# Sums of gated rows moved from the down projection of layer 1 to its up projection, and a query operand at another address

## The chip, the core and the metric

The kernel runs on one core of a Trainium2 chip. A core has a matrix engine (TensorE, PE in the profile), a vector engine (VectorE, DVE), a scalar engine (ScalarE, ACT), a general engine (GpSimd, POOL), a queue engine that here only issues transfers (SyncE, SP), an on-chip memory for operands (SBUF), accumulators that the matmuls write (PSUM), and DMA engines that move data between DRAM and SBUF. The metric is the device time of one execution in microseconds, the median of the runs.

## What is computed

Two transformer layers over 1024 tokens of width 1024, with 256 context tokens, in fp32. Layer 0 has a local attention, layer 1 grouped-query attention with rotary positions; both end in the same gated MLP with a depthwise convolution of width 3 over the tokens (2816 hidden channels per half, so 22 tiles of 128):

```python
def conv_ffn(x, w_up, conv_w, conv_b, w_down):
    h = x @ w_up
    h = lax.conv_general_dilated(h, conv_w[:, None, :], window_strides=(1,), padding=((1, 1),), ...
                                 feature_group_count=h.shape[-1]) + conv_b
    a, g = jnp.split(h, 2, axis=-1)
    return (jax.nn.silu(g) * a) @ w_down

for layer in range(DEPTH):
    xm = modulate(h, g_pre_m, sh_m, sc_m)
    y, yc = odd_mixer(...) if layer % 2 else even_mixer(...)
    h = h + gt_m * rms_norm(y, g_post_m)
    f = conv_ffn(modulate(h, g_pre_f, sh_f, sc_f), w_up[layer], conv_w[layer], conv_b[layer], w_down[layer])
    h = h + gt_f * rms_norm(f, g_post_f)
```

## The kernel before

The core works through the layers in order: attention, its output projection, up projection, down projection. In the last layer no context rows are carried, and only that layer is touched by the change.

**Precision.** An fp32 operand is split into a rounded part (hi) and the rest (lo); a product of two such operands is three matmuls, hi·hi, hi·lo, lo·hi. ScalarE casts the hi part (L121) and VectorE subtracts for the lo part (L122).

**Up projection** (`ffn_up`). It makes 22 hidden tiles j = 0 to 21, each of 128 channels by 1024 tokens, for the linear half and the gate half. Both halves together are written as a 2×2 block matrix and multiplied in seven half-sized products instead of eight: per tile 7 products × 4 blocks × 3 = 84 matmuls of 512 columns. The seven products need sums of weight blocks; GpSimd makes these, four operations of 128×512 per tile, into the single-buffered tile `sw` (L460, L461, L463, L464). VectorE adds up products (L479, L572), does the convolution in four steps of 128×1023 (L518, L519), and multiplies by the activated gate (L579); ScalarE starts the convolution and applies silu (L578). The tile is then stored to DRAM as `hid` j, 512 KB (L580, on SP's queue; the last tile's on ScalarE's).

**Down projection** (`ffn_down`). It multiplies hid with w_down by the same seven-product scheme. Its inner dimension is cut into three chunks of 3, 4 and 4 block pairs; the pair k consists of hid k and hid k + 11, each halved by tokens, which gives four blocks of 128×512: a11, a12 (first token half) and a21, a22 (second). They are loaded back from DRAM (L668, 256 KB each). In each chunk the products run in the order 1, 2, 5, 6, 7, 3, 4. Products 1, 2, 4 take plain blocks; 5, 6, 7, 3 take sums of them, made in place by GpSimd one product ahead, one operation of 128×512 per pair and product:

```python
def summed(name, s, i, e):
    if s:
        x, y, plus = s
        e.tensor_tensor(res[name][i], res[x][i], res[y][i], op=ALU.add if plus else ALU.subtract)   # L686
```

These are a21 + a22 for product 5, that minus a11 for 6, a12 minus the latter for 3, and a11 − a21 for 7. The sum is written over a block that an earlier product has split. Each product has four PSUM tiles of 4 (or 3) × 3 × 4 matmuls; ScalarE copies some of them out (L785, L796), VectorE adds the others to the rows y (L738 and like it), and GpSimd makes some additions of y in SBUF.

**Order.** A scheduler with a timeline of its own sets each engine's order from the program and its dependences; it runs before execution and the result is a fixed list for each engine. SP issues its loads and stores in that list's order and waits at each for its buffer or its data: weights (`wraw`, L445; `xm` for w_down, L653), hid stores and loads. Within the lists, what is written earlier in the program tends to stand earlier, and each engine executes strictly in its order.

**Attention of layer 1** (`odd_attn`). For each block of queries the scores are two accumulating matmuls per key tile (L1703): the keys' hi part with Q, and a second key operand with `q2`. `load_q2` (L1655) loads q2's lower 64 partitions; the tile is [128, 4, 128], 2048 bytes a partition, in three buffers.

Of the kernel before, what the change touches and what calls it, by code (L numbers as in the profile page):

```python
# [10 lines left out]
F32R = mybir.dt.float32r  # L11
AF = mybir.ActivationFunctionType
ALU = mybir.AluOpType
# [4 lines left out]
P = 128  # L18
T = 1024
# [8 lines left out]
NH = DFF // P  # L28
HF = 512
# [26 lines left out]
class Net:  # L56
# [415 lines left out]

        return [first, lambda: sums(1), lambda: sums(2), lambda: part(load(NH + j) if ctx else load(NH + j)[:, HF:])]

    def ffn_up(self, l, ctx, pre, zb, pool, side=None):

        nc = self.nc
        V, G = nc.vector, nc.gpsimd
        add = lambda o, x, y, e=V: e.tensor_tensor(o, x, y, op=ALU.add)  # L479
        order = [(0, 0), (0, 3)] if ctx else [(0, 0)]  # L480
        order += [(j, 0) for j in range(1, pre)]
        order += [(j, i) for j in range(NH) for i in range(4) if (j, i) not in order]
        steps = [self.up_weights(l, j, ctx, pool, 2 <= j < pre) for j in range(NH)]
        ready, state = {}, {}
        X, Xc = {}, []

# [37 lines left out]
        def one(j):  # L524

            a = take(j, 0)
            p1 = product(a[0], "B11")
            za = zt()
            nc.scalar.copy(za[:, HF:], p1)  # L529
            p2 = product(a[1], "B21")  # L530
            add(za[:, :HF], p2, za[:, HF:])
            oa = og = d = None
            rest = lambda: None
            if ctx:
                def rest():
                    conv(oa[:, T:], plain(a), j)
                if j == 0 or j >= pre:
# [47 lines left out]
        def run(X_, Xc_, hook1, hook2):  # L585
            X.update(X_)
            Xc.extend(Xc_ or [])
            for j in range(pre):
                one(j)
            for j in range(NH):  # L590
                if j >= pre:
                    one(j)
                if side:
                    self.steps(side, 1 if j % 4 else 2)
                if j == NH - 1:
                    hook1()
                two(j, hook2 if j == NH - 1 else None)

        return lambda: ahead(2), run

# [28 lines left out]
            self.tc.keep_in_program_order(nc.sync.dma_start(self.tD[l][k], r))  # L629
            yield  # L630

    def ffn_down(self, l, ctx, A, blocks, units):


        nc = self.nc
# [3 lines left out]
        chunks = [range(x, y) for x, y in zip(self.CUT, self.CUT[1:])]  # L639
        res = {}  # L640
        cnt = [0, 0, 0]

        def load_b(c, nm, pin):
            f = int(nm[1]) - 1
# [13 lines left out]
        def weights(n):  # L658

            if n < len(items):  # L660
                load_b(items[n][0], self.FORM[items[n][1]][1], 4 <= n < 7)

        def load_a(c, nm):
            r, h = int(nm[1]) - 1, int(nm[2]) - 1
            res[nm] = []
            for i, k in enumerate(chunks[c]):
                x = blocks(nm, i)
                nc.sync.dma_start(x, self.hidD[k + h * (NH // 2)][:, r * HF:(r + 1) * HF])  # L668
                res[nm].append(x)
            if ctx:  # L670
                n = len(chunks[c])
                x = blocks(nm, 4)[:, :n * P]
                nc.sync.dma_start(x.rearrange("p (k n) -> p k n", k=n), self.hidC[c][h][:, r])
                res[nm].append(x)

        def prep(c, nm):

            a, b, asum = self.FORM[nm]
            n = len(chunks[c])
            nu = n + (1 if ctx else 0)  # L680
            o = ops[c, nm] = [None] * nu, [None] * n

            def summed(name, s, i, e):
                if s:
                    x, y, plus = s
                    e.tensor_tensor(res[name][i], res[x][i], res[y][i], op=ALU.add if plus else ALU.subtract)  # L686

# [49 lines left out]
        def run(src, dst, sink):  # L737
# [101 lines left out]
            for n, (c, nm) in enumerate(items):  # L839
# [4 lines left out]
                for p in range(np_):  # L844
                    if p == 4:
                        for f in early + late:
                            f()
                        early = late = []
                    cnt[2] += 1
                    o = self.t(*((self.by, [P, HF], "by") if cnt[2] % 6 < 4 else (self.bj, [P, HF], "bj")))  # L850
                    multiply(o, c, nm, p, 0, len(chunks[c]))
                    collect(c, nm, p, o)
# [26 lines left out]
    def mlp(self, xa, opA, l, ctx, yT, w_out, src, mid, dst, ahead=None, after=None):  # L879
# [5 lines left out]
        A = lambda: self.t(xa, [P, HF], "xm", 16, F32R)  # L885
        mod = self.mod_cols(l, 1)
        halves = lambda x: x.rearrange("p (x n) -> p x n", x=2)
        with ExitStack() as e0:
            pool = lambda name, e: e.enter_context(tc.tile_pool(name=f"{name}{l}", reuse_waits="tile", bufs=1))
            xb = pool("xb", e0)  # L890

# [6 lines left out]
            with self.banks(out=4, turn=2):  # L898
              with self.banks(junk=1, tmp=1):
                with ExitStack() as e1:  # L900
                  xb2 = pool("xd", e1)
                  E = lambda dt=F32: self.t(xb2, [P, HF], "xd", 16, dt)
                  with ExitStack() as e2:
# [31 lines left out]
                      start, run = self.ffn_up(l, ctx, 2 if ctx else 6, 3 if ctx else 7, lambda: up[0], side)  # L935

                      def rows(n):
                          res = []
# [45 lines left out]
                  load_w, load_h, down = self.ffn_down(l, ctx, A, blocks, units)  # L984
                  with ExitStack() as e3:
                      up.append(pool("up", e3))

# [663 lines left out]

    def load_q2(self, pool, p, h, q):

        q2 = self.t(pool, [P, 4, P], "q2", 3, F32R)
        self.nc.sync.dma_start(q2[0:64].bitcast(F32), self.qP[p][0:64, h:h + 4, q * P:(q + 1) * P])  # L1655
        return q2

# [250 lines left out]
```

## Time and profile before

| | |
|---|---|
| median of 3 runs | 2901.68 us (2897.69 to 2901.73) |
| the profiled execution | 2902.14 us, span 2900.3 us, mean granted TensorE clock 0.989 |

Stages of the profiled execution, us from the span's start, with the busy time of each engine:

| stage | window | length | PE | DVE | ACT | POOL |
|---|---|---|---|---|---|---|
| attention, layer 1 | 1710 to 2133 | 423 | 413.87 | 330.33 | 232.57 | 372.46 |
| its output projection | 2133 to 2225 | 92 | 91.32 | 53.33 | 56.20 | 41.31 |
| up projection, layer 1 | 2225 to 2656 | 431 | 421.50 | 373.34 | 191.30 | 165.81 |
| down projection, layer 1 | 2656 to 2900 | 244 | 217.74 | 231.74 | 101.93 | 161.20 |

How to read the lines that follow: an instruction's row in the timeline is its start in us, its duration, engine, source line, operation, output and inputs by the program's names, shape, how many were joined, and in brackets how long its engine had been idle and what ended that. A group's row ends with the busy sum, the mean of one in ns, and the idle time before them. A row of the waits is the waiting engine, its tile and line, the engine and line that ended the wait, then the sum in us, the number, and the longest. A window's row has each engine's busy us (and count), the granted TensorE clock (1.00 is full), the busy share of the DMA engines and GB/s.

### The profile page before, as it was taken

What the parts mean: (1) busy time and instruction counts of PE and PEld (TensorE: products, weight loads), DVE (VectorE), ACT (ScalarE), POOL (GpSimd) and SP (SyncE); (2) the same over time, 40 slices, a digit from 0 to 9 for tenths busy, and PEclk for the clock granted to TensorE, in tenths of its full rate; (3) what the DMA queues carried; (4) which work ended last, traced back from release to release, by engine and by line L of the source; (5) the groups of instructions that cost most, each with busy time, mean ns of one, the idle gap of its engine ahead of it and who ended that gap; (6) DMA issues with size and microseconds to landing.
All of it is one profiled execution on the core that took longest, in us unless ns stands there. A gap on an engine that the chain in (4) does not pass through costs nothing.

```text
span 2900.3 us, 42828 instructions
## 1 busy us (share of the span) xinstructions
PE 2795.5 (96%) x15699; PEld 2252.0 (78%) x15699; DVE 2125.2 (73%) x2645; ACT 1330.5 (46%) x2373; POOL 1497.5 (52%) x1396
## 2 busy tenths in 40 slices
PE   8999999999999999999989999999998999999997
PEld 6878977776888888878768986666677878887775
DVE  4451255569776777798988768888856898888999
ACT  4321066575333333444457545555556444444443
POOL 2231277446222222165767768888864543332766
PEclk9999999999999999999999999999999999999998
DMA  8366773554223333464244562232253222224642
GB/s 314 127 209 211 242 270 133 197 188 151 79 96 124 118 102 109 167 204 129 75 138 155 148 180 93 101 102 99 84 204 138 73 95 88 88 80 168 202 142 87
DMA packets 235650, 413.89 MB, mean 143 GB/s; under 512 B 28320, under 2 KB 133792, under 8 KB 227504
## 3 DMA queue, kind: packets, MB, share of 16 engines
q1 hardware_dynamic: 212736, 395.61, 40.5%
q10 hardware_dynamic: 22704, 15.55, 1.8%
q8 instruction: 124, 2.03, 0.3%
q14 instruction: 86, 0.70, 0.1%
HBM read 306.16 MB, written 104.92 MB: 142 GB/s over the span
## 4 chain that ended last, share of the span: by engine, by line
PE 55%; DVE 11%; POOL 6%; issue 4%; ACT 2%; DMA 2%; SPq 0%; DVEq 0%; POOLq 0%; ACTq 0%
PE by L500 8%; PE by L501 8%; PE by L502 8%; PE b L1703 4%; PE by L1715 4%; PE b L1684 3%; PE by L877 2%; PE by L875 2%; PE by L876 2%; DVE xb L122 2%; DVE wlo L122 2%; PE by L509 1%; PE by L511 1%; PE by L510 1%; POOL rstd L139 1%
## 5 line engine op out<-in xcount | busy, mean ns | idle before, releaser
L1727 POOL TENSOR_TENSOR part<-part,pT 128x512 f32<-128x512 f32 x192 | 271.6, 1415 | 14.4 <-ACT pT L1704 1.0
L463 POOL TENSOR_TENSOR sw<-wraw,wraw 128x512 f32<-128x512 f32 x44 | 61.0, 1386 | 422.2 <-DVE wlo L122 422.2
L122 DVE TENSOR_TENSOR wlo<-wraw,whi 128x1024 fp32r<-128x1024 f32 (+1 forms) x162 | 221.1, 1371 | 77.4 <-ACT whi L121 77.3
L479 DVE TENSOR_TENSOR z<-by,z 128x512 f32<-128x512 f32 x264 | 176.7, 684 | 106.5 <-PE by L502 103.7
L1704 ACT ACTIVATE pT<-b 128x512 f32<-128x512 f32 x320 | 170.4, 604 | 151.2 <-PE b L1703 137.4
L1685 DVE TENSOR_REDUCE ng<-b 128x1 f32<-128x1280 f32 x122 | 181.7, 1490 | 75.7 <-PE b L1684 75.3
L121 ACT CAST whi<-wraw 128x1024 fp32r<-128x1024 f32 (+1 forms) x162 | 159.5, 990 | 160.8 <-PE b L310 107.0
L500 PE MATMUL by<-xb,whi 128*128 128x512 f32 x528 | 208.0, 394 | 1.7 <-ACT xb L121 1.7
L502 PE MATMUL by<-xb,wlo 128*128 128x512 f32 x528 | 205.9, 390 | 1.0 <-DVE wlo L122 1.0
L501 PE MATMUL by<-xb,whi 128*128 128x512 f32 x528 | 206.2, 391 | 0.3 <-DVE xb L122 0.3
L121 ACT CAST xb<-xb 128x512 fp32r<-128x512 f32 (+2 forms) x184 | 103.2, 567 | 195.2 <-PE by L876 61.6
L615 POOL TENSOR_TENSOR ts<-ts 128x512 f32<-128x512 f32 x88 | 118.3, 1352 | 134.9 <-DMA ts<-in_w_down_dram 133.2
L121 ACT CAST whi<-sw 128x1024 fp32r<-128x1024 f32 x88 | 92.5, 1052 | 202.6 <-PE by L501 173.6
L518 DVE SCALAR_TENSOR_TENSOR o<-z,cw,o 128x1023 f32<-128x1023 f32 x88 | 141.2, 1605 | 48.7 <-ACT o L517 48.6
L122 DVE TENSOR_TENSOR xb<-xb,xb 128x512 fp32r<-128x512 f32 (+2 forms) x184 | 158.9, 879 | 19.4 <-ACT xb L121 18.2
L517 ACT ACTIVATE o<-z,cw 128x1024 f32<-128x1024 f32 x88 | 109.6, 1245 | 130.5 <-DVE z L479 109.0
L460 POOL TENSOR_TENSOR sw<-wraw 128x512 f32<-128x512 f32 x44 | 80.6, 1832 | 167.6 <-DVE wlo L122 124.7
L738 POOL TENSOR_TENSOR y<-y,wraw 128x512 f32<-128x512 f32 x72 | 116.2, 1636 | 94.0 <-DVE wraw L738 59.3
L1715 PE MATMUL by<-pT,Vs 128*64 128x256 f32 x1280 | 150.7, 382 | 0.0
L500 PE MATMUL by<-xm,whi 128*128 128x512 f32 x352 | 138.5, 393 | 4.6 <-ACT z L529 3.2
L500 PE MATMUL by<-xd,whi 128*128 128x512 f32 x352 | 137.4, 390 | 0.4 <-DVE z L479 0.3
L501 PE MATMUL by<-xm,whi 128*128 128x512 f32 x352 | 137.5, 391 | 0.0
(314 smaller groups left out, 8922.0 us busy)
## 6 DMA issues: line engine op xcount, KB each, us to landing
wraw<-in_w_up_t_dram SPq DMA_DIRECT2D x92, 512.0 KB
awr<-in_w_ada_dram SPq DMA_DIRECT2D x44, 1024.0 KB
ts<-in_w_down_dram SPq DMA_DIRECT2D x44, 512.0 KB
tD<-ts SPq DMA_DIRECT2D x22, 1024.0 KB
xm<-tD SPq DMA_DIRECT2D x88, 256.0 KB
hid<-o SPq DMA_DIRECT2D x43, 512.0 KB
xm<-in_w_down_dram SPq DMA_DIRECT2D x66, 256.0 KB
xb<-hid SPq DMA_DIRECT2D x66, 256.0 KB
```

Source lines behind the costliest of these rows:

```text
L121: x = nc.scalar.copy(hi, src) if hi_eng == "s" else nc.vector.tensor_copy(hi, src)
L122: y = (nc.gpsimd if lo_eng == "p" else nc.vector).tensor_tensor(lo, src, hi.bitcast(F32), op=ALU.subtract)
L479: add = lambda o, x, y, e=V: e.tensor_tensor(o, x, y, op=ALU.add)
L500: nc.tensor.matmul(o, W[0][:, k, :], hi[k], start=(k == 0), stop=False)
L501: nc.tensor.matmul(o, W[0][:, k, :], lo[k], start=False, stop=False)
L502: nc.tensor.matmul(o, W[1][:, k, :], hi[k], start=False, stop=(k == 3))
L518: V.scalar_tensor_tensor(o[:, 1:], z[:, :n - 1], cw(0), o[:, 1:], op0=ALU.mult, op1=ALU.add)
L615: sub = lambda o, x, y: nc.gpsimd.tensor_tensor(o, x, y, op=ALU.subtract)
L1685: nc.vector.tensor_reduce(b["ng"][:, h:h + 1], ps[:, :S], axis=AX.X, op=ALU.max, negate=True)
L1704: nc.scalar.activation(b["pT"][:, k], ps, AF.Exp)
L1715: nc.tensor.matmul(out(b["po"][:, :256], i), self.KV[b["g"]][2][:, k], two(b["pT"][:, k], i), start=(k == 0), stop=(k == NT - 1))
L1727: nc.gpsimd.tensor_tensor(x, x if k > 1 else b["pT"][:, 0], b["pT"][:, k], op=ALU.add)
```

## The change

A generator `hidden_sums` is new. For each pair k it loads hid k and hid k + 11 into one tile `hs` of 128×2×1024 (single-buffered), makes the four sums in place with four GpSimd operations of 128×512, and stores the tile, 1 MB, to a DRAM buffer `sD` k. The up projection of layer 1 takes its tiles in the order 0, 11, 1, 12, …, 10, 21 so that pairs are complete early, and from the fourth tile on advances the generator by one or two steps per tile; the last two pairs' steps run into the down projection. There, `load_a` loads the block for product 5 from sD in place of a21, and `made` loads the blocks for products 6, 3 and 7 from sD, 33 loads of 256 KB, where GpSimd made sums before. Layer 0 is as it was. In the attention, q2's tile becomes 576 floats wide and the operand starts at its element 48, 192 bytes in.

```diff
+    def hidden_sums(self, l, pool):
+        nc = self.nc
+        e = lambda o, x, y, op=ALU.subtract: nc.gpsimd.tensor_tensor(o, x, y, op=op)
+        for k in range(NH // 2):
+            r = self.t(pool, [P, 2, T], "hs", 1)
+            for h in range(2):
+                nc.sync.dma_start(r[:, h], self.hidD[k + h * (NH // 2)])
+            yield
+            (x, y), (u, v) = ((r[:, h, :HF], r[:, h, HF:]) for h in range(2))
+            e(v, v, y, ALU.add)
+            e(y, x, y)
+            yield
+            e(x, v, x)
+            e(u, u, x)
+            nc.sync.dma_start(self.sD[l][k], r)
+            yield
+    SUM = {5: (1, 1), 7: (0, 1), 6: (0, 0), 3: (1, 0)}
...
-    def ffn_up(self, l, ctx, pre, zb, pool, side=None):
+    def ffn_up(self, l, ctx, pre, zb, pool, side=None, hs=None):
+        seq = [k + h * (NH // 2) for k in range(NH // 2) for h in range(2)] if hs else list(range(NH))
...
-                two(j, hook2 if j == NH - 1 else None)
+                late = hs and n > 2
+                if late and n % 2 == 0:
+                    next(hs)
+                two(j, hook2 if n == NH - 1 else None)
+                if late:
+                    next(hs)
...
+        def made(x, k, nm):
+            h, r = self.SUM[nm]
+            nc.sync.dma_start(x, sD[k][:, h, r * HF:(r + 1) * HF])
...
-                nc.sync.dma_start(x, self.hidD[k + h * (NH // 2)][:, r * HF:(r + 1) * HF])
+                if sD and nm == "a21":
+                    made(x, k, 5)
+                else:
+                    nc.sync.dma_start(x, self.hidD[k + h * (NH // 2)][:, r * HF:(r + 1) * HF])
...
-                if s:
+                if s and sD and i < n:
+                    if nm != 5:
+                        made(res[name][i], chunks[c][i], nm)
+                elif s:
...
+                    if hs and cnt[2] % 2:
+                        next(hs, None)
...
-        q2 = self.t(pool, [P, 4, P], "q2", 3, F32R)
+        q2 = self.t(pool, [P, 4 * P + 64], "q2", 3, F32R)[:, 48:48 + HF].rearrange("p (h q) -> p h q", h=4)
```

The instructions' order is the same on every engine up to the up projection of layer 1; inside it, it moves on POOL and SP alone; from its end on, on all of them. Line numbers below the new generator are 25 to 43 higher after.

**In the up projection, GpSimd.** Two tiles of the steady part; `sw` are the weight sums, `hs` the new tile. Before:

```order
L461 TENSOR_TENSOR sw_23145<-sw_23145,wraw_23123 128x512
L463 TENSOR_TENSOR sw_23145<-wraw_23123,wraw_23143 128x512
L464 TENSOR_TENSOR sw_23145<-wraw_23123,sw_23145 128x512
L460 TENSOR_TENSOR sw_23282<-wraw_23280 128x512
L461 TENSOR_TENSOR sw_23282<-sw_23282,wraw_23260 128x512
L463 TENSOR_TENSOR sw_23282<-wraw_23260,wraw_23280 128x512
```

After:

```order
L460 TENSOR_TENSOR sw_23462<-wraw_23460 128x512
L461 TENSOR_TENSOR sw_23462<-sw_23462,wraw_23440 128x512
L479 TENSOR_TENSOR hs_23684<-hs_23684 128x512
L463 TENSOR_TENSOR sw_23462<-wraw_23440,wraw_23460 128x512
L464 TENSOR_TENSOR sw_23462<-wraw_23440,sw_23462 128x512
L479 TENSOR_TENSOR hs_23684<-hs_23684 128x512 x3
L460 TENSOR_TENSOR sw_23602<-wraw_23600 128x512
L461 TENSOR_TENSOR sw_23602<-sw_23602,wraw_23580 128x512
L463 TENSOR_TENSOR sw_23602<-wraw_23580,wraw_23600 128x512
```

One new sum stands between the second and third weight sum of a tile, three more behind the tile's fourth, and the next tile has none.

**In the up projection, SP's queue.** `wraw` are the weights of a tile, `hid` its store, `hs` the load back for the sums, `sD` their store. Before:

```order
L580 DMA hid_7_4196_20886<-o_23059 128x1024
L445 DMA wraw_23280<-in_w_up_t_dram 128x1024
L445 DMA wraw_23397<-in_w_up_t_dram 128x1024
L580 DMA hid_8_4197_20887<-o_23196 128x1024
L445 DMA wraw_23417<-in_w_up_t_dram 128x1024
L445 DMA wraw_23534<-in_w_up_t_dram 128x1024
L580 DMA hid_9_4198_20888<-o_23333 128x1024
```

After:

```order
L605 DMA hid_5_4194_20884<-o_23513 128x1024
L483 DMA hs_23966<-hid_5_4194_20884 128x1024
L445 DMA wraw_23742<-in_w_up_t_dram 128x1024
L445 DMA wraw_23862<-in_w_up_t_dram 128x1024
L605 DMA hid_16_4205_20895<-o_23653 128x1024
L483 DMA hs_23966<-hid_16_4205_20895 128x1024
L445 DMA wraw_23882<-in_w_up_t_dram 128x1024
L445 DMA wraw_24004<-in_w_up_t_dram 128x1024
L492 DMA sD_5_4223_20915<-hs_23966 128x2048
L605 DMA hid_6_4195_20885<-o_23795 128x1024
```

Each tile's store is now followed by its load back, which waits for that store, and the next weights stand behind; one store of 1 MB comes per pair.

**At the end of the up projection, VectorE.** The last tile's convolution (o, z), last gate (o with o), and splits for the down projection: `xb` of hid blocks, `whi` and `wlo` of w_down. Before:

```order
L122 TENSOR_TENSOR xb_5013_25130<-xb_4987_25054,xb_5012_25129 128x512
L122 TENSOR_TENSOR wlo_25111<-xm_24914,wlo_25111 128x512
L122 TENSOR_TENSOR xb_5010_25115<-xb_4986_25052,xb_5009_25114 128x512
L572 TENSOR_TENSOR z_24982<-z_24982,by_25017 128x512
L518 SCALAR_TENSOR_TENSOR o_25013<-z_24888,cw_597,o_25013 128x1023
L122 TENSOR_TENSOR xb_5016_25145<-xb_4988_25056,xb_5015_25144 128x512
L519 SCALAR_TENSOR_TENSOR o_25013<-z_24888,cw_597,o_25013 128x1023
L518 SCALAR_TENSOR_TENSOR o_25031<-z_24982,cw_597,o_25031 128x1023
L519 SCALAR_TENSOR_TENSOR o_25031<-z_24982,cw_597,o_25031 128x1023
L122 TENSOR_TENSOR wlo_25239<-xm_24922,wlo_25239 128x512
L579 TENSOR_TENSOR o_25013<-o_25013,o_25031 128x1024
```

After:

```order
L122 TENSOR_TENSOR xb_4994_25065<-xb_4985_25045,xb_4993_25064 128x512
L122 TENSOR_TENSOR wlo_25202<-xm_25000,wlo_25202 128x512
L597 TENSOR_TENSOR z_25068<-z_25068,by_25103 128x512
L543 SCALAR_TENSOR_TENSOR o_25099<-z_24974,cw_597,o_25099 128x1023
L122 TENSOR_TENSOR xb_5034_25224<-xb_5008_25143,xb_5033_25223 128x512
L544 SCALAR_TENSOR_TENSOR o_25099<-z_24974,cw_597,o_25099 128x1023
L543 SCALAR_TENSOR_TENSOR o_25117<-z_25068,cw_597,o_25117 128x1023
L122 TENSOR_TENSOR xb_5031_25206<-xb_5007_25141,xb_5030_25205 128x512
L122 TENSOR_TENSOR xb_5037_25239<-xb_5009_25145,xb_5036_25238 128x512
L544 SCALAR_TENSOR_TENSOR o_25117<-z_25068,cw_597,o_25117 128x1023
L122 TENSOR_TENSOR wlo_25338<-xm_25008,wlo_25338 128x512
L604 TENSOR_TENSOR o_25099<-o_25099,o_25117 128x1024
```

The splits of the three blocks a12 of product 2 (before xb_4986 to 4988, after xb_5007 to 5009) stand otherwise among the steps L518 and L519 (L543 and L544 after): before, two ahead of the first step and one behind it; now all three behind it, two of them right ahead of the last step.

**At the down projection's sixth product in the first chunk, ScalarE.** Casts of hid blocks (`xb`) and weights, and the copies of product 5's PSUM tiles into y. Before, a_0 to a_2 are the blocks of product 6, summed by GpSimd, xb_4963 one of product 7, xb_4986 one of product 3:

```order
L121 CAST xb_5041_25262<-a_0_4989_25058 128x512
L121 CAST whi_25336<-xm_25081 128x512
L121 CAST xb_5044_25277<-a_1_4990_25060 128x512
L121 CAST wlo_25396<-xm_25148 128x512
L121 CAST xb_5058_25340<-xb_4963_24955 128x512
L121 CAST xb_5075_25420<-xb_4986_25052 128x512
L796 COPY y_0_4996_25072<-by_25228 128x512
L796 COPY y_1_4997_25073<-bj_25247 128x512
L796 COPY y_2_4998_25074<-bj_25266 128x512
L121 CAST xb_5047_25292<-a_2_4991_25062 128x512
L796 COPY y_3_4999_25075<-by_25281 128x512
```

After, a_0 to a_2 are the blocks of product 6, loaded from sD, and xb_5007 to 5009 those of product 3:

```order
L839 COPY y_0_5017_25161<-by_25327 128x512
L839 COPY y_1_5018_25162<-bj_25346 128x512
L839 COPY y_2_5019_25163<-bj_25365 128x512
L121 CAST xb_5097_25519<-xb_5007_25141 128x512
L121 CAST wlo_25495<-xm_25242 128x512
L121 CAST xb_5100_25535<-xb_5008_25143 128x512
L839 COPY y_3_5020_25164<-by_25380 128x512
L121 CAST whi_25499<-xm_25244 128x512
L121 CAST xb_5063_25361<-a_0_5010_25147 128x512
L121 CAST xb_5066_25376<-a_1_5011_25149 128x512
L121 CAST xb_5069_25391<-a_2_5012_25151 128x512
```

The casts of a_0 and a_1 stood ahead of the copies and that of a_2 ahead of the last one; now all three stand behind the last copy and one cast of weights, and two casts for product 3 stand ahead of them.

More of the change, by code (lines that the diff above doesn't have):

```diff
@@ L480, in ffn_up @@
         order = [(0, 0), (0, 3)] if ctx else [(0, 0)]
-        order += [(j, 0) for j in range(1, pre)]
-        order += [(j, i) for j in range(NH) for i in range(4) if (j, i) not in order]
-        steps = [self.up_weights(l, j, ctx, pool, 2 <= j < pre) for j in range(NH)]
+        order += [(j, 0) for j in seq[1:pre]]
+        order += [(j, i) for j in seq for i in range(4) if (j, i) not in order]
+        steps = {j: self.up_weights(l, j, ctx, pool, 2 <= n < pre) for n, j in enumerate(seq)}
         ready, state = {}, {}
@@ L536, in rest @@
                     conv(oa[:, T:], plain(a), j)
-                if j == 0 or j >= pre:
+                if j == 0 or j not in seq[:pre]:
                     oa = ot()
@@ L587, in run @@
             Xc.extend(Xc_ or [])
-            for j in range(pre):
+            for j in seq[:pre]:
                 one(j)
-            for j in range(NH):
-                if j >= pre:
+            for n, j in enumerate(seq):
+                if n >= pre:
                     one(j)
                 if side:
-                    self.steps(side, 1 if j % 4 else 2)
-                if j == NH - 1:
+                    self.steps(side, 1 if n % 4 else 2)
+                if n == NH - 1:
                     hook1()
-                two(j, hook2 if j == NH - 1 else None)
+                late = hs and n > 2
[4 more added lines that the diff above has]
+                    next(hs)
         return lambda: ahead(2), run
@@ L630, in down_sums, with ffn_down @@
             yield
-    def ffn_down(self, l, ctx, A, blocks, units):
+    def ffn_down(self, l, ctx, A, blocks, units, hs=None):
         nc = self.nc
@@ L641, in ffn_down @@
         cnt = [0, 0, 0]
+        sD = self.sD.get(l)
         def load_b(c, nm, pin):
@@ L887, in mlp @@
         halves = lambda x: x.rearrange("p (x n) -> p x n", x=2)
+        self.sD = {}
         with ExitStack() as e0:
+            hsum = None
+            if not ctx:
+                self.sD[l] = [self.t(self.dr, [P, 2, T], f"sD{l}_{k}") for k in range(NH // 2)]
+                hsum = self.hidden_sums(l, e0.enter_context(tc.tile_pool(name=f"hs{l}", reuse_waits="tile", bufs=1, side="right")))
             pool = lambda name, e: e.enter_context(tc.tile_pool(name=f"{name}{l}", reuse_waits="tile", bufs=1))
@@ L934, in mlp @@
                                                 acc=lambda: self.t(self.bj, [P, HF], "bj"), turn=lambda: self.t(self.bt, [P, 512], "b1"))
-                      start, run = self.ffn_up(l, ctx, 2 if ctx else 6, 3 if ctx else 7, lambda: up[0], side)
+                      start, run = self.ffn_up(l, ctx, 2 if ctx else 6, 3 if ctx else 7, lambda: up[0], side, hsum)
                       def rows(n):
@@ L983, in mlp @@
                   units = Units(lambda i: B(where[i]), len(where) // 2)
-                  load_w, load_h, down = self.ffn_down(l, ctx, A, blocks, units)
+                  load_w, load_h, down = self.ffn_down(l, ctx, A, blocks, units, hsum)
                   with ExitStack() as e3:
```

## The prediction, made before the changed kernel ran

> **What bounds the kernel now.** I read the page first, then the stages' windows, then what TensorE waits for in the last stage, then each of those waits in the timeline.
>
> ```profile
> PE 2795.5 (96%) x15699; PEld 2252.0 (78%) x15699; DVE 2125.2 (73%) x2645; ACT 1330.5 (46%) x2373; POOL 1497.5 (52%) x1396
> ```
> ```profile
> core 0: us, PE busy (x) PEld busy (x) DVE busy (x) ACT busy (x) POOL busy (x), PEclk, DMA share, GB/s
> 2440.40:2630.20 189.80, 189.80 (x839) 157.17 (x838) 159.12 (x161) 78.15 (x80) 63.75 (x40) 1.00 0.23 81
> 2656.00:2900.00 244.00, 217.74 (x928) 176.35 (x926) 231.74 (x260) 101.93 (x197) 161.20 (x112) 0.95 0.45 149
> 2660.00:2680.00 20.00, 16.54 (x66) 12.95 (x65) 17.31 (x19) 10.44 (x18) 6.32 (x4) 0.91 0.45 144
> 2680.00:2700.00 20.00, 17.63 (x76) 13.89 (x75) 20.00 (x18) 11.97 (x22) 15.03 (x9) 1.00 0.84 275
> 2780.00:2800.00 20.00, 18.13 (x73) 14.51 (x72) 20.00 (x19) 4.27 (x8) 17.69 (x11) 0.91 0.43 137
> ```
>
> TensorE (PE) is the bound as long as it is fed. The second row is ten hidden tiles in the steady part of layer 1's up projection: PE is busy all of the 189.80 us, VectorE 159.12, GpSimd 63.75. The third is layer 1's down projection to the end: VectorE 231.74 of 244, PE only 217.74. So the up projection has VectorE time to spare (30.7 us in ten tiles, 6.1 per pair) and PE none; in the down projection VectorE is full and PE waits for it. PE's waits from 2656 to 2900:
>
> ```profile
> PE by L875 <- ACT y L785: 3.5, 1, 3.5
> PE by L877 <- DVE xb L122: 2.7, 3, 1.6
> PE by L876 <- DVE whi L122: 1.9, 2, 1.1
> PE bj L876 <- DVE whi L122: 1.9, 1, 1.9
> PE by L876 <- DVE wlo L122: 1.3, 1, 1.3
> ```
> ```profile
> 2668.54 0.39 PE L877 MATMUL by<-wlo,xb 128*128 128x512 f32 x1
> 2672.39 0.50 PE L875 MATMUL by<-wlo,xb 128*128 128x512 f32 x1 [3.46 <-ACT y L785]
> ...
> 2690.54 0.74 PE L877 MATMUL by<-whi,xb 128*128 128x512 f32 x2 [1.55 <-DVE xb L122]
> 2696.23 0.72 PE L877 MATMUL by<-wlo,xb 128*128 128x512 f32 x2 [0.82 <-DVE xb L122]
> ...
> 2791.97 0.50 PE L876 MATMUL bj<-whi,xb 128*128 128x512 f32 x1 [1.87 <-DVE whi L122]
> ...
> 2792.91 0.63 PE L876 MATMUL by<-wlo,xb 128*128 128x512 f32 x1
> 2793.33 0.63 PE L877 MATMUL by<-wlo,xb 128*128 128x512 f32 x1
> ```
>
> 11.3 us of waiting, and more: after the long waits the granted clock falls (0.91 in 2660:2680 and in 2780:2800, so 0.09 x 20 = 1.8 us each), and matmuls start 0.42 us apart (2792.91, 2793.33). In all some 15 us that this stage could give back; the rest is fed PE or VectorE's closing work.
>
> **The sums, where they stand now.**
>
> ```profile
> L686 POOL TENSOR_TENSOR xb<-a,a 128x512 f32<-128x512 f32 x11 | 19.2, 1744 | 0.0
> L686 POOL TENSOR_TENSOR a<-a,a 128x512 f32<-128x512 f32 x11 | 19.0, 1750 | 24.5 <-DMA a<-hid 24.5
> L686 POOL TENSOR_TENSOR a<-a,xb 128x512 f32<-128x512 f32 x11 | 18.8, 1710 | 15.0 <-DVE xb L122 15.0
> L686 POOL TENSOR_TENSOR xb<-xb,a 128x512 f32<-128x512 f32 x11 | 18.3, 1666 | 0.0
> ```
> ```profile
> 2660.37 1.28 DVE L518 SCALAR_TENSOR_TENSOR o<-z,cw,o 128x1023 f32<-128x1023 f32 x1
> 2662.17 2.32 DVE L519 SCALAR_TENSOR_TENSOR o<-z,cw,o 128x1023 f32<-128x1023 f32 x1
> 2664.41 2.31 DVE L518 SCALAR_TENSOR_TENSOR o<-z,cw,o 128x1023 f32<-128x1023 f32 x1
> 2666.75 2.19 DVE L519 SCALAR_TENSOR_TENSOR o<-z,cw,o 128x1023 f32<-128x1023 f32 x1
> 2669.04 1.06 ACT L578 ACTIVATE o<-o 128x1024 f32<-128x1024 f32 x1 [4.21 <-DVE o L519]
> 2671.38 0.33 ACTq L580 DMA_DIRECT2D hid<-o  x1
> 2671.75 1.56 ACT L785 COPY y<-by 128x512 f32<-128x512 f32 x3 [1.15 <-DVE o L579]
> 2661.76 6.10 POOL L686 TENSOR_TENSOR a<-a,a 128x512 f32<-128x512 f32 x3 [24.48 <-DMA a<-hid]
> ```
>
> 44 GpSimd operations, 75 us, not on PE's path themselves. What they do to VectorE is. The same convolution step takes 1.28 us at 2660.37 and 2.32, 2.31, 2.19 once GpSimd's three sums run beside it (2661.76, 6.10 us): about 1.0 us of VectorE lost per sum. So the 44 cost VectorE up to 45 us of the 231.74.
>
> Price by wait, gains negative:
>
> 1. The wait at 2672.39 (3.46). PE wants a PSUM buffer; ScalarE frees it (L785, 2671.75) behind the last store of hid, which waits for the last gate, which waits for those three steps. Without sums beside them they end 1.04 + 1.03 + 0.91 = 3.0 us sooner. In the new order two splits, some 0.6 each like the copies of 2671.75 (1.56 for three), stand behind the steps that stood ahead of them, no net change. 0.5 us of wait stays and most of the clock's 1.8 goes. Ends -3.0 to -5.3; I take -4.5, nearer the second, since a wait of 0.5 is like the 0.82 at 2696.23, in a window at clock 1.00.
>
> 2. The waits at 2690.54 and 2696.23 (2.4 together). Nine sums ran there, four remain (the last pair's): five at 1.0 free more VectorE time than was waited for. New instead: ScalarE's cast of product 6's operand stands behind the copy of product 5's last PSUM tile and one other cast, so PE waits for copy, cast and cast, 3 x 0.6 = 1.8 us. Net -0.6; ends -2.4 (the wait is covered) and +2 (it drops the clock too).
>
> 3. The wait at 2791.97, 1.87 plus 1.8 of clock. VectorE was full from 2680 on with 16 sums beside it; without them it has 16 us more for a delay of 1.9. -3.2; ends 0 and -3.7.
>
> 4. The remaining 3.5 us of waits, almost all in the last two products. GpSimd's eight additions of y (L738) stay beside them. -1.0; ends 0 and -3.5.
>
> 5. 33 sums become loads of 256 KB on SP's queue, written over a block that the product before has to have split.
>
> ```profile
> SPq L653 <- DMA hid<-o: 14.6, 1, 14.6
> ```
> ```profile
> 2674.01 1.27 SPq L653 DMA_DIRECT2D xm<-tD  x3
> ```
>
> The store issued at 2671.38 lets SP go on at 2674.01: 2.6 us from issue to landing for 512 KB, and I take that for a load too. A product of four blocks lasts 48 x 0.227 = 10.9 us, so a load is hidden if SP issues it in the product's first half. SP is in order, and one late load holds the weights behind it. The other 11 loads stand in place of loads of a21. +1.0; ends 0 and +5.
>
> 6. The up projection gets 40 of the 44 sums (the last pair's four run in the down projection), 20 loads of 512 KB, ten stores of 1 MB.
>
> ```profile
> 2444.34 1.29 POOL L463 TENSOR_TENSOR sw<-wraw,wraw 128x512 f32<-128x512 f32 x1 [7.90 <-DVE wlo L122]
> 2450.97 1.68 POOL L460 TENSOR_TENSOR sw<-wraw 128x512 f32<-128x512 f32 x1 [4.08 <-DVE wlo L122]
> ```
>
> GpSimd waits 7.90 and 4.08 us in each tile for VectorE to release the buffer of weight sums: one new sum falls into the first gap of one tile in two and three into the second, where 3 x 1.3 = 3.9, or 3 x 2.2 when contended. The latter delays L460 by some 2.5 us; behind it wait ScalarE's cast and a product that was prepared more than a product ahead. VectorE loses 4 x 1.04 = 4.2 us per pair and has 6.1. On SP each load of hid stands behind the store of the same tile and waits 2.6 us for it, with the next weights queued behind; before, those weights waited for GpSimd anyway. The order of tiles costs nothing: the same products, and all pairs of the first chunk are done long before. +1.0 for local lag; 0 is one end, +10 the other (1 us per pair; a gain is excluded, since PE has no wait there).
>
> 7. The query operand. No row shows addresses, so I go by starts of equal matmuls.
>
> ```profile
> 2440.29 0.39 PE L500 MATMUL by<-xb,whi 128*128 128x512 f32 x1
> 2440.51 0.39 PE L501 MATMUL by<-xb,whi 128*128 128x512 f32 x1
> ```
> ```profile
> 1905.10 0.40 PE L1703 MATMUL b<-q,k 128*128 128x512 f32 x1
> 1905.34 0.40 PE L1703 MATMUL b<-Q,k 128*128 128x512 f32 x1
> ```
>
> 0.22 to 0.23 us apart in the up projection, 0.24 in the attention. If the new place took that difference away for its 320 matmuls, 320 x 8 ns = 2.5 us; a loss of the same size I can't exclude. I take 0.
>
> Sum: -4.5 - 0.6 - 3.2 - 1.0 + 1.0 + 1.0 + 0 = -7.3. The profiled execution took 2902.14 us (span 2900.3), which gives 2894.8. The median of the runs is 0.5 lower (2901.68): **2894.4 us**.
>
> **Rivals.** A measurement of this kernel can tell 0.2%, 5.8 us, from no change.
>
> *The relief is given back* (no change). Loads of sums arrive late behind SP's in-order queue, and PE waits for casts where it waited for VectorE: term 5 at +5 and term 2 at +2 leave about -1, so 2901. For it: at 2680:2700 the DMA share is already 0.84. Against: it falls to 0.43 later. It decides if a load is issued after half a product.
>
> *VectorE becomes the bound of the up projection* (slower). It decides where four sums cost VectorE more than the 6.1 us per pair, 1.5 us each.
>
> ```profile
> L461 POOL TENSOR_TENSOR sw<-sw,wraw 128x512 f32<-128x512 f32 x15 | 32.4, 2158 | 1.2
> ```
>
> A contended GpSimd operation lasts 2158 ns; if VectorE stood still for all of that, 4 x 2.16 = 8.6, 2.5 us too much, times ten pairs +25: 2920 at the worst, 2908 at half of it. Against: 1.04 lost per sum is what 2662.17 to 2666.75 show. The Trainium skill, "SBUF — State Buffer", section "SBUF: two separate sides", speaks for it: GpSimd and a VectorE operation with two SBUF inputs take their shared ports as an exclusive lock for the whole instruction, and the other blocks fully. By that rule a sum could cost its full uncontended 1.29 us instead of 1.04: 5.2 per pair instead of 4.2, still below 6.1, so the sum stays, with less room; I give this rival a larger chance for it.
>
> *The query's place matters more* (faster): the attention's other matmuls gain too, -2.5 or more, 2892 and below.
>
> **How the numbers follow.** Forecast 0.55 (2890 to 2898; 0.48 of it beyond 5.8 us, 0.07 within), relief given back 0.22, up projection slower 0.15, query place 0.08. Faster 0.48 + 0.08 = 0.56; same 0.07 + 0.22 = 0.29; slower 0.15. Range 2888 to 2903: it takes in the given-back case whole, leaves out about 0.12 of the slow one and 0.08 below.
>
> **What would show it.** Right: no wait near 3.5 us at the first PSUM copies and none at the third chunk's start; VectorE's splits in the down projection shorter; the up projection as long as before within 2 us, its convolution steps slower. Wrong: PE waits for splits (DVE wlo, xb) inside the up projection; ScalarE's casts waiting for DMA of sD; the attention's stage longer or shorter by over 3 us.

## The result and the profile after

The changed kernel is slower: 2918.18 us (median of 4 runs, 2916.4 to 2920.66) against 2899.68 (4 runs); the ratio is 1.0067, 95% interval 1.0050 to 1.0084. The forecast was 2894.4, range 2888 to 2903.

The profiled execution has a span of 2915.2 us, 14.85 above the 2900.32 of before. I cut both at the same matmuls. A stage's length is counted from its first matmul's start to its last one's, and the down projection's from the last matmul of the up projection on. The four starts of the changed kernel:

```profile
2211.18 0.48 PE L525 MATMUL by<-xm,whi 128*128 128x512 f32 x1
2677.01 0.39 PE L527 MATMUL by<-xd,wlo 128*128 128x512 f32 x1
2677.24 0.39 PE L920 MATMUL by<-whi,xb 128*128 128x512 f32 x1
2898.85 0.39 PE L922 MATMUL by<-whi,xb 128*128 128x512 f32 x1
```

| | before | after | difference |
|---|---|---|---|
| attention, layer 1 | 413.17 | 407.39 | -5.78 |
| up projection | 437.93 | 465.83 | +27.90 |
| down projection | 228.33 | 221.83 | -6.50 |
| the rest | 1820.89 | 1820.12 | -0.77 |

So the up projection, put at +1, lost 28. The down projection came within 2 us of what the forecast's terms 1 to 5 sum to (-8.3), but by luck: a larger relief and a larger cost than forecast offset each other, as the account of terms 1 to 5 below shows. The same stretches by engine, first the up projection (437.93 and 465.83 us), then the down projection to the span's end; before:

```profile
2218.37:2656.30 437.93, 428.42 (x1880) 350.67 (x1879) 378.24 (x402) 195.41 (x234) 169.07 (x119) 0.99 0.27 95
2656.53:2900.31 243.78, 217.21 (x925) 175.94 (x923) 231.21 (x259) 101.93 (x197) 161.20 (x112) 0.95 0.44 148
```

and after:

```profile
2211.18:2677.01 465.83, 437.63 (x1880) 350.39 (x1879) 402.49 (x397) 191.57 (x235) 247.28 (x159) 0.99 0.37 132
2677.24:2915.16 237.92, 212.77 (x925) 174.34 (x923) 193.16 (x263) 101.10 (x196) 86.66 (x72) 0.96 0.59 202
```

VectorE (third busy time) went up by 24 us in the up projection for 40 sums (GpSimd has 159 operations there, 119 before), 0.6 us a sum, less than the 1.04 of the forecast; with 402 busy of 466 it is not the bound of that stage as a whole. What TensorE waits for there, in the steady part from 2400 to 2660, is this; in the kernel before no wait is seen from 2400 to 2656:

```profile
PE by L525 <- DVE z L504: 6.0, 6, 1.0
PE by L525 <- ACT whi L121: 4.4, 6, 0.9
PE by L527 <- DVE wlo L122: 3.2, 6, 0.5
```

Three waits once per pair of tiles, each at the same place. One pair, GpSimd's timeline:

```profile
2441.03 2.15 POOL L461 TENSOR_TENSOR sw<-sw,wraw 128x512 f32<-128x512 f32 x1
2453.38 1.30 POOL L479 TENSOR_TENSOR hs<-hs 128x512 f32<-128x512 f32 x1 [10.19 <-issue]
2454.63 2.27 POOL L463 TENSOR_TENSOR sw<-wraw,wraw 128x512 f32<-128x512 f32 x1
2456.87 1.28 POOL L464 TENSOR_TENSOR sw<-wraw,sw 128x512 f32<-128x512 f32 x1
2458.12 5.22 POOL L479 TENSOR_TENSOR hs<-hs 128x512 f32<-128x512 f32 x3
2463.30 2.27 POOL L460 TENSOR_TENSOR sw<-wraw 128x512 f32<-128x512 f32 x1
2465.65 2.16 POOL L461 TENSOR_TENSOR sw<-sw,wraw 128x512 f32<-128x512 f32 x1
```

SP, VectorE and TensorE beside it:

```profile
2447.16 0.33 SPq L605 DMA_DIRECT2D hid<-o  x1
2449.82 0.33 SPq L483 DMA_DIRECT2D hs<-hid  x1
```
```profile
2449.05 1.22 DVE L122 TENSOR_TENSOR wlo<-sw,whi 128x1024 fp32r<-128x1024 f32 x1
2454.04 1.72 DVE L544 SCALAR_TENSOR_TENSOR o<-z,cw,o 128x1023 f32<-128x1023 f32 x1
2459.26 1.23 DVE L122 TENSOR_TENSOR wlo<-sw,whi 128x1024 fp32r<-128x1024 f32 x1 [3.50 <-ACT whi L121]
2460.41 1.78 DVE L122 TENSOR_TENSOR wlo<-wraw,whi 128x512 fp32r<-128x512 f32 x1
2462.11 2.31 DVE L543 SCALAR_TENSOR_TENSOR o<-z,cw,o 128x1023 f32<-128x1023 f32 x1
2464.94 1.71 DVE L544 SCALAR_TENSOR_TENSOR o<-z,cw,o 128x1023 f32<-128x1023 f32 x1
2466.58 2.32 DVE L122 TENSOR_TENSOR wlo<-wraw,whi 128x1024 fp32r<-128x1024 f32 x1
```
```profile
2459.29 0.50 PE L525 MATMUL by<-xb,whi 128*128 128x512 f32 x1 [0.68 <-ACT whi L121]
2460.55 0.50 PE L527 MATMUL by<-xb,wlo 128*128 128x512 f32 x1 [0.53 <-DVE wlo L122]
2469.55 0.50 PE L525 MATMUL by<-xd,whi 128*128 128x512 f32 x1 [0.98 <-DVE z L504]
```

Read it from GpSimd. It is free at 2443.2. VectorE releases `sw` at 2450.27 (2449.05 + 1.22), and the tile's third weight sum L463 could run then. But a sum of hidden rows stands ahead of it, and that one waits for its rows: the tile's store is issued at 2447.16, the load back 2.66 us later, and the sum starts at 2453.38, 3.56 us after that. (The row names no releaser for it, only "issue"; but in nine of the ten pairs the first sum starts 3.4 to 3.6 us after its load is issued.) L463 starts at 2454.63, 4.4 us late. The cast of these weights comes late, VectorE stands idle 3.50 us for it, and TensorE waits 0.68 and 0.53 us. Then VectorE has to catch up while three sums and the next tile's L460 and L461 run beside it: its steps take 2.31, 1.71, 2.32 us, and TensorE waits 0.98 us for a PSUM tile. From start to start of their 168 matmuls, a pair of tiles lasts 41.2 us in place of 38.1.

In the down projection the waits of before are gone, all but one of 1.7 us and two under 0.4, and one is new, 7.0 us before product 6 (below it, a wait of SP's queue):

```profile
PE by L920 <- ACT xb L121: 7.0, 1, 7.0
PE by L920 <- ACT y L828: 1.7, 1, 1.7
```
```profile
SPq L685 <- DMA hid<-o: 6.2, 1, 6.2
```
```profile
2698.74 1.27 SPq L685 DMA_DIRECT2D xm<-tD  x3
2700.05 1.38 SPq L685 DMA_DIRECT2D xm<-in_w_down_dram  x3
2701.47 0.43 SPq L483 DMA_DIRECT2D hs<-hid  x1
2701.95 1.91 SPq L685 DMA_DIRECT2D xm<-tD  x3
2704.04 2.05 SPq L698 DMA_DIRECT2D a<-sD  x3
2706.43 6.65 SPq L685 DMA_DIRECT2D xm<-in_w_down_dram  x8
```
```profile
2711.35 1.97 ACT L121 CAST xb<-a 128x512 fp32r<-128x512 f32 x3 [2.66 <-DMA a<-sD]
```
```profile
2704.67 0.39 PE L922 MATMUL by<-whi,xb 128*128 128x512 f32 x1
2712.02 0.80 PE L920 MATMUL by<-wlo,xb 128*128 128x512 f32 x1 [6.96 <-ACT xb L121]
```
```profile
2704.00:2711.00 7.00, 1.06 (x5) 0.56 (x3) 5.38 (x6) 4.64 (x9) 3.01 (x3) 0.88 1.01 339
```

SP stands for 6.2 us until the last hid store has landed. Then it issues ten other loads, and product 6's three blocks are asked for from 2704.04 on, when product 5's last matmul (2704.67) is about to start. The cast that needs them starts at 2711.35, 7.3 us later. In between, from 2704 to 2711, the DMA engines are busy all the time (share 1.01) and TensorE 1.06 us of 7.

### The profile page after: what moved, and what is told of

It reads as the page before. It is cut to its first block, busy times and chain, and to the rows that moved or that the text cites. A ratio compares the mean times of both kernels' runs of the same rounds, so it can differ in the third digit from the quotient of the medians.

```text
span 2915.2 us, 42936 instructions
## 1 busy us (share of the span) xinstructions
PE 2798.1 (96%) x15699; PEld 2251.1 (77%) x15699; DVE 2106.6 (72%) x2645; ACT 1326.0 (45%) x2373; POOL 1504.2 (52%) x1396
## 4 chain that ended last, share of the span: by engine, by line
PE 50%; DVE 12%; issue 6%; POOL 6%; DMA 4%; ACT 3%; DVEq 0%; POOLq 0%; ACTq 0%; SPq 0%
PE by L525 5%; PE by L527 5%; PE by L526 5%; PE b L1754 5%; PE by L1766 4%; PE by L920 3%; PE by L922 3%; PE by L921 3%; DVE wlo L122 3%; PE b L1735 3%; DVE o L543 2%; PE bj L920 1%; PE bj L921 1%; PE bj L922 1%; PE by L534 1%
## 5 line engine op out<-in xcount | busy, mean ns | idle before, releaser
L122 DVE TENSOR_TENSOR wlo<-wraw,whi 128x1024 fp32r<-128x1024 f32 (+1 forms) x162 | 235.8, 1461 | 79.4 <-ACT whi L121 79.4
L463 POOL TENSOR_TENSOR sw<-wraw,wraw 128x512 f32<-128x512 f32 x44 | 68.0, 1545 | 340.7 <-DVE wlo L122 340.7
L504 DVE TENSOR_TENSOR z<-by,z 128x512 f32<-128x512 f32 x264 | 176.5, 683 | 89.4 <-PE by L527 86.2
L1736 DVE TENSOR_REDUCE ng<-b 128x1 f32<-128x1280 f32 x122 | 181.9, 1491 | 75.6 <-PE b L1735 75.3
L543 DVE SCALAR_TENSOR_TENSOR o<-z,cw,o 128x1023 f32<-128x1023 f32 x88 | 142.6, 1621 | 49.4 <-ACT o L542 49.2
L460 POOL TENSOR_TENSOR sw<-wraw 128x512 f32<-128x512 f32 x44 | 84.4, 1917 | 133.9 <-DVE wlo L122 91.8
```

Source lines behind the costliest of these rows:

```text
L122: y = (nc.gpsimd if lo_eng == "p" else nc.vector).tensor_tensor(lo, src, hi.bitcast(F32), op=ALU.subtract)
L543: V.scalar_tensor_tensor(o[:, 1:], z[:, :n - 1], cw(0), o[:, 1:], op0=ALU.mult, op1=ALU.add)
L1736: nc.vector.tensor_reduce(b["ng"][:, h:h + 1], ps[:, :S], axis=AX.X, op=ALU.max, negate=True)
```

## The experiments

Twelve runs. "Attention", "up" and "down" are the lengths in us of the three stages in the run's profile, cut as in the table above. The ratio is the run's time to that of the kernel before, measured beside it, with its 95% interval. Line numbers are those of each run's own kernel. First the cause in the up projection and the place of q2, each part alone.

**q2_only**: the kernel before with

```diff
-        q2 = self.t(pool, [P, 4, P], "q2", 3, F32R)
+        q2 = self.t(pool, [P, 4 * P + 64], "q2", 3, F32R)[:, 48:48 + HF].rearrange("p (h q) -> p h q", h=4)
```

> The kernel before with the moved query operand alone. Between the first and the last score matmul the attention of layer 1 took 413.2 us before and 407.4 after the whole change. Theory (the place of q2 gives this): attention 407 to 408, all else as before, time 5 to 6 us below before. Rival (only the matmuls that follow q2 gain, 3.3 ns each, 320 of them): 1 us less, not distinguishable from before. Rival (chance between executions): attention 412 to 414.

Attention 407.1; ratio 0.9983 (0.9973 to 0.9992). This looked like the theory; the later runs below say otherwise.

**sums_only**: the changed kernel with that line as before.

> The changed kernel with q2 back in its old place: the sums' move alone. Theory: up projection (first to last matmul) 466 us against 437.9 before, down projection (from there to the last matmul) 222 against 228.3, attention 413: time 20 to 22 us above before. Rival (q2's place gives nothing): 15 to 18 above, as the whole change.

Ratio 1.0085 (1.0069 to 1.0100), which is 25 us of 2899 (20 to 29), at or above the 20 to 22 of the theory and more than the rival's 15 to 18. Up 468.1, down 222.1 as in the whole change, and attention 409.5, shorter than the 413.2 of before although q2 is in its old place. So the loss is the sums' move, and something other than q2 moves the attention's time.

**behind**: all four sums of a pair pinned behind the last weight sum.

```diff
-                nc.gpsimd.tensor_tensor(s1, A12, s1, op=ALU.subtract)
+                self.sw_last = nc.gpsimd.tensor_tensor(s1, A12, s1, op=ALU.subtract).ins
...
-            e(v, v, y, ALU.add)
-            e(y, x, y)
+            with self.tc.issue_after(self.sw_last):
+                e(v, v, y, ALU.add)
+                e(y, x, y)
```

> The changed kernel with all four sums of a pair queued behind the tile's last weight sum, so that the first of them, which waits for its load, no longer stands ahead of two weight sums. Theory (the wait for the load ahead of the weight sums costs 0.86 + 0.69 = 1.55 us per pair, the sums' contention with VectorE 1.15): up projection 466 - 15 = about 451 us. Rival (VectorE's lost time alone is the cause): 466, unchanged. Rival (SP's queue delays weights): 466, unchanged.

Up 455.0, ratio 1.0028 (1.0018 to 1.0038). The steady pairs went from 41.2 to 39.1 us, so the wait ahead of the weight sums cost 2.05 us a pair, more than the 1.55 read off the waits; two of the first tiles got 2 to 3 us longer, which is why the stage gained 10.9 and not 15. Both rivals expected no change. From 2400 to 2660 only VectorE's lateness is left, about one wait per pair:

```profile
PE by L526 <- DVE z L505: 5.5, 7, 1.0
PE by L528 <- DVE wlo L122: 0.8, 1, 0.8
```

Yet VectorE is busy for longer than in the changed kernel, 414.86 us against 402.49, in a stage that is 10.9 us shorter, so the time that VectorE loses in all does not set the stage's length:

```profile
2208.52:2663.49 454.97, 432.71 (x1881) 350.93 (x1879) 414.86 (x398) 192.54 (x235) 257.04 (x159) 0.99 0.39 135
```

**no_sums**: the loads and stores stay, the GpSimd operations go.

```diff
-            e(v, v, y, ALU.add)
-            e(y, x, y)
...
-            e(x, v, x)
-            e(u, u, x)
```

> The changed kernel without the four GpSimd operations of a pair: the loads of hid and the stores to sD stay, so sD holds plain rows and the result is not the reference's. Theory and the rival of VectorE's lost time: up projection 438 to 440 us, as before. Rival (loads and stores on SP's queue delay the weights): 460 to 466. The down projection keeps its wait of 7 us for the loads of product 6 if that is a matter of the loads; if it is due to the last pair's sums, it goes.

Up 437.7, ratio 0.9947 (0.9934 to 0.9959). The 20 loads, ten stores and the new order of tiles cost TensorE nothing; all 28 us come from the GpSimd operations. The down projection (218.8) kept a wait of 6.7 us for product 6's cast: that one is a matter of the loads.

Then the two repairs, alone and together.

**spread**: two sums behind the last weight sum of one tile, two behind the first two of the next. The generator also starts one tile earlier and takes two steps per pair instead of three.

```diff
-                nc.gpsimd.tensor_tensor(s1, s0, A11, op=ALU.subtract)
+                self.sw_mid = nc.gpsimd.tensor_tensor(s1, s0, A11, op=ALU.subtract).ins
...
+            with self.tc.issue_after(self.sw_last):
                 e(v, v, y, ALU.add)
                 e(y, x, y)
             yield
+            with self.tc.issue_after(self.sw_mid):
                 e(x, v, x)
                 e(u, u, x)
             nc.sync.dma_start(self.sD[l][k], r)
-            yield
...
-                late = hs and n > 2
-                if late and n % 2 == 0:
-                    next(hs)
+                if hs and n > 1:
+                    next(hs)
                 two(j, hook2 if n == NH - 1 else None)
-                if late:
-                    next(hs)
```

> The changed kernel with the same sums of a pair in two halves: two behind the last weight sum of one tile, two behind the first weight sums of the next tile, where GpSimd waits longest. All four queued together behind the last weight sum left the up projection at 455.0 us against 437.7 without the sums, 1.05 us per pair in the steady part. Theory (what remains is VectorE late at one place, since three to four sums run beside it in a row): with two at a time its spare time of 3.1 us per tile covers them, up projection 440 to 445, time near 2895. Rival (each sum costs TensorE in proportion, wherever it stands): 455, as with four together.

Up 448.0; ratio 1.0004 (0.9994 to 1.0014). In the steady part no wait for another engine is left, and a pair lasts 38.6 us in place of 38.1. The stage still misses the forecast by 3 to 8 us: tiles four to seven, counted from zero at 84 matmuls in a row each, take 86.8 us against 79.8 before.

**early6**: the changed kernel, product 6's sums loaded into the blocks of a22, which are free from the start of the chunk, and a22 loaded behind product 6.

```diff
-                if sD and nm == "a21":
-                    made(x, k, 5)
+                if sD and nm in ("a21", "a22"):
+                    made(x, k, 5 if nm == "a21" else 6)
...
-                    if nm != 5:
+                    if nm in (7, 3):
...
+            if sD and nm == 6:
+                a = "a22"
...
+                elif sD and nm == 4 and i < n:
+                    nc.sync.dma_start(res[name][i], self.hidD[chunks[c][i] + NH // 2][:, HF:])
```

> The changed kernel with the loads of product 6 into the block of a22, free long before, and a22 itself (needed by product 4) loaded behind product 6. Theory (the wait of 7.0 us before product 6's matmuls comes from its loads, which stand in SP's queue behind loads that wait, and then share the DMA engines): the wait goes and with it the clock's loss behind it, down projection 222 - 7 to 9 = 213 to 215 us, time 2909 to 2911. Rival (the loads are late wherever they go, since the DMA engines are full): a wait of 5 us or more stays, 220 to 222.

Down 212.6, ratio 1.0039 (1.0027 to 1.0051). The wait of 7.0 is gone, and what is left of TensorE's waits in the whole stage is

```profile
PE by L924 <- ACT y L832: 1.7, 1, 1.7
PE by L926 <- DVE xb L122: 0.3, 1, 0.3
PE bj L926 <- DVE xb L122: 0.3, 1, 0.3
```

SP now issues the three loads of the first chunk with three others from 2692.28 on, ahead of its wait for the last hid store and of the ten loads behind that. 9.2 us from product 6's loads issued earlier: 7.1 between two matmul starts (2704.67 and 2712.02, over the usual 0.227), and 2.1 of slow starts that followed.

**spread6**: both.

> Both of the above. Theory: up projection 440 to 445, down projection 213 to 215, attention 407: time 2884 to 2890, 10 to 15 us below before. Rival (the gains meet in one place, the start of the down projection): no better than the first of the two, near 2895.

Up 448.0, down 212.6, as the two alone; ratio 0.9989 (0.9980 to 0.9997). The time, 2899.0, is above the 2884 to 2890 expected. The up projection stayed above 440 to 445, and the kernel before took 2903.6 beside it, so the gain is some 3 us (1 to 6) and not 10 to 15. The profiled execution, with 415.1 us of attention, took 2902.85.

**before_nosum**: what the sums cost in the down projection, with nothing in exchange.

```diff
-                if s:
+                if s and (l == 0 or i >= n):
```

> The kernel before without GpSimd's 44 sums in the down projection of layer 1 and nothing in their place: products 5, 6, 7 and 3 use the plain blocks, so the result is not the reference's. It shows what the sums cost there, without any loads in exchange. Theory of the prediction (terms 1 to 4 without the new casts: 4.5 + 2.4 + 3.2 + 1.0): down projection 228.3 - 11 = 217 us, up to 15 less at the most, 213; time 2885 to 2889. Rival (TensorE's waits there come from elsewhere): over 224.

Down 210.1, ratio 0.9951 (0.9939 to 0.9962): 18.3 us, more than the 11 to 15 of the theory. The only wait left is one of 0.3 us. So the sums cost more there than I had put, and with early6 the moved version has all but 2.6 us of that relief.

Then q2's place again, with controls.

**before_again** is the kernel before unchanged, **q2_again** repeats q2_only, **q2_wide** has the wider tile with the operand at its start:

```diff
-        q2 = self.t(pool, [P, 4, P], "q2", 3, F32R)
+        q2 = self.t(pool, [P, 4 * P + 64], "q2", 3, F32R)[:, 0:0 + HF].rearrange("p (h q) -> p h q", h=4)
```

> The kernel before, unchanged, as one more sample. Up to here the attention of layer 1 lasted 409.5 to 414.4 us in three traces with q2's old place and 407.1 to 415.1 in seven with the new, in steps of about 1.0 us: single blocks of 12.7 us last 13.7, when TensorE waits for VectorE's maximum (L1685), in 0 to 9 of the 31 blocks. Theory (the number of such blocks changes from execution to execution, the place has little to do with it): attention anywhere from 407 to 415. Rival (the place matters): 409 or more.

> The run with q2 moved alone, once more. First time: attention 407.1, time 0.9983 of before. Theory (chance): attention anywhere from 407 to 415, ratio 0.998 to 1.001. Rival (the place is worth 3 to 6 us): ratio again 0.998 to 0.999, attention 407 to 409.

> The tile of 576 floats with the operand at its start, so the place modulo 256 is the old one and only the tile's size is new. If the place matters: ratio 1.000, attention 409 or more, matmul starts behind q2 232.8 ns apart as before instead of 229.5. If it is the layout of the tiles behind it or chance: like the run with q2 moved.

Ratios 1.0002 (0.9991 to 1.0013), 1.0002 (0.9992 to 1.0012) and 0.9997 (0.9986 to 1.0009); attention 409.7, 408.5 and 410.6. The gain of the first run with q2 moved (5 us) did not come again (+1 us). Over all traces the attention took 409.5 to 414.4 us in five with the old place and 407.1 to 415.1 in nine with the new. Five of the nine, 407.1 to 408.5, lie below all five of the old place, and one lies above them, so a gain of one or two us is neither shown nor excluded. What differs is how often TensorE waits for VectorE's maximum; here the changed kernel and then spread6, with the same attention code and q2 in the same new place (a line of the attention is 51 higher in the changed kernel than before, more than the 25 to 43 given above, so L1736 is L1685 of before):

```profile
PE b L1735 <- DVE ng L1736: 4.2, 4, 1.3
```
```profile
PE b L1737 <- DVE ng L1738: 10.0, 12, 1.5
```

The place does have an effect, in the starts of matmuls: the matmul on Q that follows one on q2 comes 232.6 to 232.9 ns after it in the five traces with the old place and 229.0 to 229.6 in the nine with the new (means of 194 such pairs in each). 3.3 ns by 194 is 0.6 us, too little for the times to show. In the some 50 pairs where a matmul on the keys follows, 232.6 to 234.5 ns with the old place stand against 233.8 to 235.1 with the new, no gain.

**late6**: spread6 with the generator started five tiles later, so that the sums begin where the tiles have come to their steady length, and the last four pairs in the down projection among GpSimd's additions of y.

```diff
-                if hs and n > 1:
+                if hs and n > 6:
...
-                    if hs and cnt[2] % 2:
+                    if hs and cnt[2] > 16 and cnt[2] % 2:
+                        self.pin_sums = True
...
+                i = e(v, v, y, ALU.add)
+                if self.pin_sums:
+                    self.tc.keep_in_program_order(i)
```

> The better version (sums in halves, product 6 loaded early) with the first sums from the eighth tile on instead of the fourth, and those of the last four pairs in the down projection, spread among GpSimd's additions. In the better version the tiles four to seven took 87 us, 79.6 before, since their second products are only 15 us apart; the steady pairs cost 0.5 us each. Theory: up projection 441 to 443 instead of 448, down projection 213 plus up to 5 for twelve more sums there: 213 to 218, time 2 to 6 us below that version. Rival (a sum costs the same in all tiles): no gain, 2899 or more at a time before of 2903.

Up 441.5, down 213.4, ratio 0.9974 (0.9963 to 0.9985): 2893.9 against 2900.2, the version furthest ahead of the kernel before, by 4 to 11 us. In both stages the forecast's numbers came, with the twelve more sums in the down projection costing 0.8 us, not 5.

## Why the prediction was wrong

**Term 6, the up projection, failed: +1.0, with +10 as its far end, was +27.9.** It priced the first new sum by its duration, "falls into the first gap", and looked for a delay only behind the three others. Further on it says that the load of hid waits 2.6 us for the store; it follows that wait to the weights on SP and not to GpSimd, where the sum that needs the rows stands ahead of L463 and L464. In the gap of 7.90 us there was room for the sum's 1.3 us, but not at the time when its rows were there. What the runs put in place of the +1.0: 10.9 us for that order (behind), 7.0 more that go when the sums run two at a time (spread), 6.6 when the first tiles are spared (late6, at 0.8 in the down projection), and 3.5, 0.5 a pair, that stay and that no wait in the trace explains. Its sentences on loads, stores and the order of tiles held: they cost nothing (no_sums).

**"VectorE loses 4.2 us per pair and has 6.1" was right and did not protect.** It lost less, 0.6 us per sum in the changed kernel and 0.9 in behind. But spare time in a stage is no cover at a place: VectorE idled 3.50 us for late weights and then was late by 0.98. The rival that was slower, VectorE as the bound of the up projection, gave +25 at its worst; that this is near what came is luck, since its mechanism is not seen. It needed more than 6.1 us of VectorE lost per pair, and 24 to 37 us for ten pairs are 2.4 to 3.7. By the rule of the Trainium skill that it leaned on ("SBUF — State Buffer", section "SBUF: two separate sides") a sum costs up to 1.29 us of VectorE, by the prediction's estimate; the mean of 0.6 to 0.9 here lies below it. Where one sum meets one step with two SBUF inputs, the trace agrees, to within 0.2 us, that one stands until the other is done: the sum ends at 2454.68, L544, started at 2454.04, takes 1.72 in place of the 1.27 it takes alone and ends at 2455.76, and L463, started at 2454.63, takes 2.27 in place of 1.29 and ends 1.14 us after that. VectorE's additions L504, which read a product from PSUM, take 0.67 to 0.69 us each time, also the 51 of 129 in the up projection that run beside a GpSimd operation.

**Terms 1 to 4, the relief, were right in kind and too small together.** Taking what is over 0.227 us between two matmul starts, term 1's wait went from 3.6 with 1.7 of slow starts behind it to 2.0 (-3.3, taken -4.5); term 2's two waits of 1.7 and 1.0 went to 0.9 elsewhere (-1.8, taken -2.4 before its new casts); term 3's 2.0 and 1.7 of slow starts went wholly (-3.7, taken -3.2; from 2680 to its wait at 2791.97 there were 25 sums beside VectorE and not 16); term 4's waits went, some 6 us with the slow starts among them that it had left out (taken -1.0, end -3.5).

**Term 5, the loads, was the second miss: +1.0, end +5, was +9.2.** The wait came before product 6, where term 2 had put 1.8 for casts; its cause is the loads (early6 takes all 9.2 away). Two assumptions broke. A load was priced at 2.6 us from one store that was nearly alone, and these took 7.3 with the DMA engines full; even the load of hid in the up projection, with a DMA share of 0.44, took 3.6. And "hidden if SP issues it in the product's first half" was not followed through SP's queue, where the three loads stand behind a wait of 6.2 us, nine loads of xm and one of hs, and are issued at the end of product 5. The rival that the relief is given back had named this, late loads of sums with casts waiting for them, and a load issued after half a product as the condition; it came true in one product, at more than its +5. The 9.2 ate most of the relief of terms 1 to 4, which is why the stage's -6.5 looks like the forecast's -8.3.

**Term 7, q2, is not told apart from 0**; the starts of matmuls show at most 0.6 us of it. Of the prediction's signs of being wrong two were right: TensorE waits for wlo inside the up projection, and ScalarE's casts wait for the loads of sD. The third, "the attention's stage longer or shorter by over 3 us", misled: the stage differs by up to 8 us between profiles of kernels with the same attention code, and by 3.5 between the two of the kernel before. Whether a program's layout has a part in that beside chance was not tried.

## What to carry to other kernels

When work is moved into another engine's gap, ask when its operands arrive, not only how long it runs: in an in-order engine everything behind it inherits that wait. Spare time read from a stage's window covers a cost only where it is spent, so put new work in at most the amounts that one gap holds, and away from the places where that engine is already late. And before a difference of a few us in a stage is put down to an edit, look at how much that stage varies with the edit undone.

## What was not expected of the hardware

Three loads of 256 KB took 7.3 us from issue to use while the DMA share was 1.01 (339 GB/s), against 2.6 for one store of 512 KB with less beside it (share 0.49, 199 GB/s). The attention of layer 1 varied by 8 us over 14 profiles, in single blocks of 12.7 us that take 13.7. And a matmul on Q starts 3.3 ns sooner behind one on q2 when q2 begins 192 bytes into its tile and not at its start; with the tile of the same width and the operand at its start (q2_wide) it does not (232.6 ns), so it is the place and not the tile's size. Why is open.
